# Weight sums two per projection step, and every on-chip pool at a multiple of 256 bytes

## The chip, the cores and the metric

The kernel runs on one core of one Trainium2 chip. The metric is the device time of one execution in microseconds; of several timed executions the median is given. The core has TensorE (PE, with its weight loads as PEld), VectorE (DVE), ScalarE (ACT) and GpSimd (POOL). SyncE (SP) issues nearly all loads from DRAM to the on-chip memory SBUF; POOL issues the DRAM-to-DRAM transfers of this kernel and a few small loads. All transfers run on the same 16 DMA engines, those of SP as queue q1 and those of POOL as queue q0.

## The reference, cut to what matters

One backbone layer on 512 latent tokens of width 1024, with 256 context tokens in front:

```
mod = silu(c) @ w_ada + b_ada            # six vectors: sh1, sc1, ga1, sh2, sc2, ga2
h   = modulate(rmsnorm(x), sh1, sc1)
x_a, b_a, c_a, q, k, v, r, lr_f, lr_b, gate_a, gate_b = split(h @ w_in + b_in)
y_a = (b_a * conv3(c_a * x_a)) @ w_conv_out
y_b = (rmsnorm(gla_bidir(q, k, v, ...)) * silu(r)) @ w_gla_out
y   = sigmoid(gate_a) * y_a + sigmoid(gate_b) * y_b
x   = x + ga1 * (y @ w_o)
x   = x + ga2 * (square(relu(modulate(rmsnorm(x), sh2, sc2) @ w_up)) @ w_down)
out = rmsnorm(x)
```

All data is float32. The MLP is 1024 to 4096 to 1024.

## The kernel before, in words

**Products.** Every operand of a large product is split into a high part (rounded to the fast float32 format, by ACT) and a low part (the rest, by DVE), and `mm3` makes three matmuls of it: high x high, high x low, low x high. A projection step is 8 blocks of the contraction, so 24 matmuls of 128 rows x 512 columns into one PSUM bank.

**Weights.** `weights(name, src)` takes a raw tile (`raw`, 4 of them, 4 KB per partition), lets SP load 512 KB into it (L125), and splits it into `h_<name>` (ACT) and `l_<name>` (DVE), of which there are 5 each. `Stream` asks for weights up to three steps ahead (`ahead` 3). Most weights are taken as columns, so each of their transfers is 1024 runs of 512 bytes.

**Order around the change.** `projections()` is a generator that yields after each of its 57 steps (i = 0 to 56): the 14 steps of the v and context keys, a query, 26 steps for the convolution branch (xa, c, b in turn, with two queries), 8 gates (`ga`), 8 of `co`. After each step the main loop (L923 to L928) advances the attention (`att`), then the weight sums (`sums`), and from step 44 on the second modulation (`mods`). The 16 steps of `gates()` (`r`, then `gb`) advance `mods` and `sums` too. A planner orders each engine's instructions by its own estimate of times; `pinned` ones keep the order of the program.

**Weight sums.** The down projection uses seven block products in place of eight, and so needs sums of quarters of `w_down`. `weight_sums()` makes them in DRAM, with 64 transfers of 512 KB that POOL issues: 16 copies from `w_down` (numbers 1 to 16), 16 accumulating transfers (17 to 32), then twice 8 copies of a sum into another (33 to 40 and 49 to 56) and 8 accumulating ones (41 to 48 and 57 to 64). Ahead of each stands a tiny copy (`tick`, L466) that reads the low part of the weights last asked for, so POOL waits at it, in order, until DVE has made that part:

```
for i, p, src, add in todo:
    pinned(nc.gpsimd.tensor_copy(out=tick, in_=latest[0][0:1, 0:1].bitcast(F32)))
    pinned(nc.gpsimd.dma_start(out=t_sum[i][p], in_=src, ...))       # accum_op add where add
    yield
```

`SUMS = (0, 1)` makes none at step 0 and one at each later step, 56 in `projections()`; the other 8 are made in `gates()`, one per step.

**Second modulation.** `ada_sum(i)` loads eight 512 KB blocks of `w_ada` (`wa`, L754) into the same four raw tiles as the weights, and DVE multiplies and adds them into two accumulators. `second_mods()` does so for shift 2, scale 2 and gate 1; a short product with a matrix of ones (`ps_ar`) then spreads the row over the partitions.

**Where the tiles lie.** The pools are laid one behind the other in each partition's memory: `const`, `wp` (raw, high and low weights), `kp` (the latent and MLP activations in split form, and 16 blocks of 2 KB), `sp` (columns of statistics, 1152 bytes), and `bp` (36 blocks of 2 KB), in whose place `mp` comes at the MLP. `const` begins 128 bytes past a multiple of 256 and takes 2976 bytes with each tile padded to 32. So `wp` and `kp`, whose sizes are multiples of 256, begin 32 bytes past a multiple of 256, and `bp` and `mp` 160 bytes past one. Every matrix operand of 512 columns starts at its pool's remainder.

Of the kernel before, what the change touches and what calls it, by code (L numbers as in the profile page):

```python
# [8 lines left out]
F32 = mybir.dt.float32  # L9
# [6 lines left out]
P = 128  # L16
# [23 lines left out]
NBLK = 36  # L40
NKEEP = 16
MODS_FROM = 44
SUMS = (0, 1)
UP_ORDER = [16 * j + 4 * g + i for g in range(4) for j in range(2) for i in range(4)]
TABLES = "natural_log_exp_and_others"

# [2 lines left out]
def hybrid_block_kernel(  # L49
# [9 lines left out]
    w_up, w_down, b_in, b_ada, out = w_up[0], w_down[0], b_in[0], b_ada[0], out[0]  # L59

    const = es.enter_context(tc.tile_pool(name="const", bufs=1))
    wp = es.enter_context(tc.tile_pool(name="wp", bufs=NW))
    kp = es.enter_context(tc.tile_pool(name="kp", bufs=NKEEP))
    sp = es.enter_context(tc.tile_pool(name="sp", bufs=4))
    pp = es.enter_context(tc.tile_pool(name="pp", bufs=8, space=bass.MemoryType.PSUM))
    dp = es.enter_context(tc.tile_pool(name="dp", bufs=1, space=bass.MemoryType.DRAM))

# [382 lines left out]

    t_sum = [[dp.tile([P, 2, 512], F32, tag=f"t{i}_{p}", name=f"t{i}_{p}") for p in range(NFF // 4)] for i in range(4)]
    tick = const.tile([1, 1], F32, name="tick")

    def quarter(j, hf, p):
        return rows(w_down, 16 * j + 2 * p, 512 * hf)

    def weight_sums():

        groups = range(NFF // 4)
        todo = [(i, p, quarter(0, i, p), False) for p in groups for i in range(2)]  # L460
        todo += [(i, p, quarter(i, 1, p), True) for p in groups for i in range(2)]
        for i, j, hf in ((2, 1, 1), (3, 1, 0)):
            todo += [(i, p, t_sum[(0, 2)[i - 2]][p], False) for p in groups]
            todo += [(i, p, quarter(j, hf, p), True) for p in groups]
        for i, p, src, add in todo:
            pinned(nc.gpsimd.tensor_copy(out=tick, in_=latest[0][0:1, 0:1].bitcast(F32)))  # L466
            pinned(nc.gpsimd.dma_start(out=t_sum[i][p], in_=src, **({"accum_op": ALU.add} if add else {})))  # L467
            yield
# [306 lines left out]
    def all_attention():  # L775
        for h in range(HEADS):
            yield from attention(h)
# [3 lines left out]
    def second_mods():  # L781
        yield from ada_sum(3)
        ps = psum("ps_ac")
        for k in range(KT):
            pe.matmul(ps[:, k:k + 1], ada[3][k // 4][:, (k % 4) * P:(k % 4 + 1) * P], ones[:, 0:1], start=True, stop=True)
        dve.tensor_copy(out=sh2, in_=ps[:, 0:KT])
        yield
        yield from ada_rows(4)
        for hf in range(2):
            g2 = blk("g2")  # L790
            nc.gpsimd.dma_start(out=g2, in_=g_norm2[0][hf * 512:(hf + 1) * 512].partition_broadcast(P))
            dve.scalar_tensor_tensor(out=ada[4][hf], in0=ada[4][hf], scalar=1.0, in1=g2, op0=ALU.add, op1=ALU.mult)
        yield from ada_rows(2)
# [110 lines left out]
    def gates():  # L904

        for j in range(KT):
            ps = project("r")
            rg = blk("rg")
            pinned(act.activation(out=rg, in_=ps, func=AF.Silu, bias=cb(40 + j)))
            pst = transposed("ps_ot", o_tok, j)  # L910
            dve.scalar_tensor_tensor(out=rg, in0=pst, scalar=ca(80 + j), in1=rg, op0=ALU.mult, op1=ALU.mult)
            og.append((blk(f"ogh_{j}", F32R), blk(f"ogl_{j}", F32R)))
            split(rg, *og[j])
            yield
        for j in range(KT):
            ps = project("gb")
            gb.append(kblk("gb"))
            pinned(act.activation(out=gb[j], in_=ps, func=AF.Sigmoid, bias=cb(56 + j)))
            yield
        pinned(nc.scalar.preload_act_table_set(TABLES))  # L920

    att, mods, sums = all_attention(), second_mods(), weight_sums()
    for i, _ in enumerate(projections()):  # L923
        next(att, None)
        for _ in range(SUMS[min(i, len(SUMS) - 1)]):
            next(sums, None)
# [3 lines left out]
        next(mods, None)  # L930
    for _ in gates():
        next(mods, None)
        next(sums, None)
    for _ in mods:
        pass
    for _ in sums:
# [291 lines left out]
```

## Time and profile before

| | us |
|---|---|
| median of 3 timed runs | 1000.24 (999.66 to 1001.4) |
| the profiled execution, whole | 1002.8 |
| its span, first to last instruction | 1001.0 |
| PE busy in it | 963.0 |
| DVE, ACT, POOL busy in it | 637.0, 487.8, 109.2 |
| mean granted PE clock | 0.989 of full speed |

Times of the trace count from the first instruction. A row of a timeline is start, duration, engine, line, operation, output <- inputs, count, and in brackets how long the engine sat idle before it and what ended that. Most rows name L81, the line of a helper through which all engines are called, so tiles tell more than lines. In the chain of waits a row is start, duration, engine and tile, and xN the number of instructions merged in it. PE instructions overlap, so the pace of a stream is the length of such a piece divided by its count.

### The profile page before, as it was taken

What the parts mean: (1) busy time and instruction counts of PE and PEld (TensorE: products, weight loads), DVE (VectorE), ACT (ScalarE), POOL (GpSimd) and SP (SyncE); (2) the same over time, 40 slices, a digit from 0 to 9 for tenths busy, and PEclk for the clock granted to TensorE, in tenths of its full rate; (3) what the DMA queues carried; (4) which work ended last, traced back from release to release, by engine and by line L of the source; (5) the groups of instructions that cost most, each with busy time, mean ns of one, the idle gap of its engine ahead of it and who ended that gap; (6) DMA issues with size and microseconds to landing.
All of it is one profiled execution on the core that took longest, in us unless ns stands there. A gap on an engine that the chain in (4) does not pass through costs nothing.

```text
span 1001.0 us, 13478 instructions
## 1 busy us (share of the span) xinstructions
PE 963.0 (96%) x4999; PEld 783.9 (78%) x4999; DVE 637.0 (64%) x1076; ACT 487.8 (49%) x862; POOL 109.2 (11%) x195
## 2 busy tenths in 40 slices
PE   3999999999999998799989999999999999999996
PEld 2678888778888887688878888898888888888875
DVE  5366676887688767666547354776332225699896
ACT  4465454645655474533334432374444344655662
POOL 7001021222211131002220000000000000000000
PEclk9999999999999999899989999999999999999998
DMA  9893154787664666855987425237533334555561
GB/s 264 231 289 127 33 190 138 164 169 164 144 167 146 172 129 154 244 169 175 251 205 235 129 98 171 61 89 234 162 85 105 95 116 142 192 179 191 179 211 42
DMA packets 160241, 161.22 MB, mean 161 GB/s; under 512 B 7268, under 2 KB 126160, under 8 KB 159920
## 3 DMA queue, kind: packets, MB, share of 16 engines
q1 hardware_dynamic: 146672, 123.89, 41.4%
q0 software_dynamic: 12928, 35.43, 15.1%
q10 hardware_dynamic: 576, 1.05, 0.3%
q8 instruction: 39, 0.64, 0.3%
q14 instruction: 26, 0.21, 0.1%
HBM read 158.25 MB, written 35.65 MB: 194 GB/s over the span
## 4 chain that ended last, share of the span: by engine, by line
PE 90%; DMA 4%; DVE 3%; SPq 1%; ACT 1%; issue 1%; DVEq 0%; ACTq 0%
PE ps_up L81 16%; PE ps_da L81 7%; PE ps_v L81 7%; PE ps_b L81 4%; PE ps_y L81 4%; PE ps_c L81 4%; PE ps_db L81 4%; PE ps_go L81 4%; PE ps_xa L81 4%; PE ps_gb L81 4%; PE ps_co L81 4%; PE ps_r L81 4%; PE ps_ga L81 2%; PE ps_dc L81 2%; DMA r_co<-in_w_conv_out_dram 2%; PE ps_k L81 2%
## 5 line engine op out<-in xcount | busy, mean ns | idle before, releaser
L81 DVE TENSOR_TENSOR l_up<-r_up,h_up 128x1024 fp32r<-128x1024 f32 x32 | 39.2, 1224 | 84.8 <-ACT h_up L81 84.7
L81 PE MATMUL ps_up<-h2h,l_up 128*128 128x512 f32 x232 | 90.3, 389 | 0.0
L81 PE MATMUL ps_up<-h2l,h_up 128*128 128x512 f32 x232 | 90.3, 389 | 0.0
L81 PE MATMUL ps_up<-h2h,h_up 128*128 128x512 f32 x232 | 90.3, 389 | 0.0
L81 DVE TENSOR_TENSOR l_dn<-r_dn,h_dn 128x1024 fp32r<-128x1024 f32 x56 | 68.4, 1222 | 27.1 <-ACT h_dn L81 26.9
L81 ACT CAST h_up<-r_up 128x1024 fp32r<-128x1024 f32 x32 | 33.6, 1053 | 78.8 <-PE ps_up L81 67.9
L81 ACT CAST h_dn<-r_dn 128x1024 fp32r<-128x1024 f32 x56 | 58.7, 1048 | 16.1 <-PE ps_up L81 16.1
L81 ACT CAST aph<-ug 128x512 fp32r<-128x512 f32 x56 | 34.8, 621 | 58.8 <-PE ps_da L81 25.6
L81 DVE SCALAR_TENSOR_TENSOR acc<-wa,silu_c,acc 128x512 f32<-128x512 f32 x64 | 45.4, 747 | 8.4 <-DMA wa<-in_w_ada_dram 8.2
L81 PEld LDWEIGHTS ps_up<-h2l,h_up 128*128 128x128 f32 x232 | 43.5, 188 | 9.1
L81 PEld LDWEIGHTS ps_up<-h2h,l_up 128*128 128x128 f32 x232 | 43.5, 188 | 9.0
L81 PEld LDWEIGHTS ps_up<-h2h,h_up 128*128 128x128 f32 x232 | 43.5, 188 | 9.0
L81 DVE TENSOR_TENSOR apl<-ug,aph 128x512 fp32r<-128x512 f32 x56 | 38.6, 689 | 13.5 <-ACT aph L81 13.2
L467 POOL DMA_DIRECT2D t<-in_w_down_dram x48 | 42.7, 905 | 3.8 <-issue 3.8
L81 PE MATMUL ps_da<-h_dn,aph 128*128 128x512 f32 x96 | 37.9, 395 | 0.0
L81 PE MATMUL ps_da<-h_dn,apl 128*128 128x512 f32 x96 | 37.9, 395 | 0.0
L81 PE MATMUL ps_da<-l_dn,aph 128*128 128x512 f32 x96 | 37.9, 394 | 0.0
L81 PE MATMUL ps_co<-yah,h_co 128*128 128x512 f32 x64 | 26.5, 413 | 0.0
L81 PE MATMUL ps_r<-hh,h_r 128*128 128x512 f32 x64 | 26.4, 412 | 0.0
L81 PE MATMUL ps_v<-h_v,hh 128*128 128x512 f32 x64 | 26.0, 406 | 0.0
L81 PE MATMUL ps_r<-hh,l_r 128*128 128x512 f32 x64 | 25.8, 402 | 0.0
L81 PE MATMUL ps_r<-hl,h_r 128*128 128x512 f32 x64 | 25.7, 401 | 0.0
(464 smaller groups left out, 2794.5 us busy)
## 6 DMA issues: line engine op xcount, KB each, us to landing
t<-in_w_down_dram POOLq DMA_DIRECT2D x48, 512.0 KB, 7.6
wa<-in_w_ada_dram SPq DMA_DIRECT2D x32, 512.0 KB, 4.8
r_up<-in_w_up_dram SPq DMA_DIRECT2D x32, 512.0 KB, 4.1
r_dn<-t SPq DMA_DIRECT2D x32, 512.0 KB, 3.5
r_dn<-in_w_down_dram SPq DMA_DIRECT2D x24, 512.0 KB, 3.6
wa<-in_w_ada_dram SPq DMA_DIRECT2D x32, 256.0 KB, 5.1
t<-t POOLq DMA_DIRECT2D x16, 512.0 KB, 5.3
r_v<-in_w_in_dram SPq DMA_DIRECT2D x8, 512.0 KB, 5.2
```

The costliest lines, as they stand in the source:

```text
L81: ins = op(*args, **kwargs)
L467: pinned(nc.gpsimd.dma_start(out=t_sum[i][p], in_=src, **({"accum_op": ALU.add} if add else {})))
```

## The change

After the change the main loop asks for no sum at step 0, for one at step 1 and for two at each later step. All 64 are then asked for by step 33, ahead of step 44 where the second modulation begins, and `gates()` asks for none. `sp` moves ahead of `wp`, and a pad of 96 bytes is added to `const`, which then takes 3072 bytes; `sp` with its 1152 bytes follows, so `wp`, `kp`, `bp` and `mp` all begin at multiples of 256 bytes.

```diff
-SUMS = (0, 1)
+PAD = 24
+SUMS = (0, 1, 2)
...
     const = es.enter_context(tc.tile_pool(name="const", bufs=1))
+    sp = es.enter_context(tc.tile_pool(name="sp", bufs=4))
     wp = es.enter_context(tc.tile_pool(name="wp", bufs=NW))
     kp = es.enter_context(tc.tile_pool(name="kp", bufs=NKEEP))
-    sp = es.enter_context(tc.tile_pool(name="sp", bufs=4))
...
     tick = const.tile([1, 1], F32, name="tick")
+    const.tile([P, PAD], F32, name="pad")
...
     for _ in gates():
         next(mods, None)
-        next(sums, None)
```

## Rows read from the trace of the kernel before

**Rows 1.** Page: mean busy share of the DMA engines, in tenths, 40 slices of 25 us

```profile
DMA  9893154787664666855987425237533334555561
```

**Rows 2.** PE timeline of the co and r stages, rows with idle time in brackets

```profile
386.44 0.69 PE L81 MATMUL ps_sl<-qt,kt 128*64 128x64 f32 x16 [1.76 <-DVE kt L81]
...
388.72 0.58 PE L81 MATMUL ps_s<-vcl,kwh 128*128 128x256 f32 x1 [1.28 <-DVE vcl L81]
...
414.67 1.12 PE L81 MATMUL ps_sl<-qt,kt 128*64 128x64 f32 x16 [5.01 <-DVE kt L81]
...
504.65 0.80 PE L81 MATMUL ps_ar<-ah,ones_r 128*128 128x512 f32 x1 [2.81 <-ACT ah L81]
```

**Rows 3.** ACT timeline of the same stages

```profile
382.81 1.05 ACT L81 CAST h_co<-r_co 128x1024 fp32r<-128x1024 f32 x1 [7.79 <-DMA r_co<-in_w_conv_out_dram]
...
410.70 1.04 ACT L81 CAST h_co<-r_co 128x1024 fp32r<-128x1024 f32 x1 [10.80 <-DMA r_co<-in_w_conv_out_dram]
...
489.83 1.05 ACT L81 CAST h_r<-r_r 128x1024 fp32r<-128x1024 f32 x1 [8.21 <-DMA r_r<-in_w_in_dram]
```

**Rows 4.** Windows: us, busy (x instructions) of PE, PEld, DVE, ACT, POOL, PEclk, DMA share, GB/s

```profile
398.60:402.00 3.40, 3.40 (x17) 2.81 (x16) 3.40 (x8) 1.30 (x3) 0.50 (x1) 1.00 0.86 186
...
422.50:429.30 6.80, 6.80 (x44) 5.26 (x43) 6.75 (x14) 4.22 (x9) 0.94 (x2) 1.00 0.34 96
...
514.70:521.40 6.70, 6.70 (x35) 5.53 (x32) 4.80 (x7) 3.72 (x6) 1.25 (x2) 1.00 0.75 159
```

**Rows 5.** DMA issues in 374:383, then in 395:411: count, size, median us to landing

```profile
r_co<-in_w_conv_out_dram SPq DMA_DIRECT2D x1, 512.0 KB, 8.6
...
r_co<-in_w_conv_out_dram SPq DMA_DIRECT2D x3, 512.0 KB, 10.9
```

**Rows 6.** DMA issues of the page, one weight of the convolution branch

```profile
r_c<-in_w_in_dram SPq DMA_DIRECT2D x8, 512.0 KB, 4.4
```

**Rows 7.** DMA queues: packets, MB, share; stretches 376:377, 490.5:492.5, 486:489 in turn

```profile
q0 software_dynamic: 96, 0.20, 109.8%
...
q1 hardware_dynamic: 1229, 0.62, 110.5%
...
q0 software_dynamic: 253, 0.49, 87.5%
q1 hardware_dynamic: 255, 0.17, 24.2%
```

**Rows 8.** POOL timeline, first and last tick of steps 13 to 17

```profile
164.43 1.04 POOL L466 COPY tick<-l_c 1x1 f32<-1x1 f32 x1 [30.32 <-DVE l_c L81]
...
181.53 0.24 POOL L466 COPY tick<-l_b 1x1 f32<-1x1 f32 x1 [6.12 <-DVE l_b L81]
```

**Rows 9.** SP timeline, the load of the query weights that comes next

```profile
165.46 0.37 SPq L125 DMA_DIRECT2D r_q<-in_w_in_dram  x1
```

**Rows 10.** ACT timeline, the casts of this load and of the xa behind it

```profile
185.33 1.03 ACT L81 CAST h_q<-r_q 128x1024 fp32r<-128x1024 f32 x1
...
191.37 1.05 ACT L81 CAST h_xa<-r_xa 128x1024 fp32r<-128x1024 f32 x1 [2.78 <-PE ps_b L81]
```

**Rows 11.** DVE, then PE timeline: a head's scores behind that cast

```profile
195.76 0.69 DVE L81 TENSOR_TENSOR kt<-kt,k 128x512 f32<-128x512 f32 x1
...
198.17 0.69 PE L81 MATMUL ps_sl<-qt,kt 128*64 128x64 f32 x16
```

**Rows 12.** Chain that ended last, long PE pieces: start, us, tile, matmuls

```profile
520.86 43.55 PE ps_gb L81 x192
565.34 44.62 PE ps_go L81 x192
609.95 33.60 PE ps_y L81 x144
...
730.19 0.93 PE ps_ar L81 x4
...
834.48 22.31 PE ps_db L81 x96
```

## The prediction

> **What bounds the kernel now.** I read the page first: of a span of 1001.0 us PE is busy for 963.0, and the DMA engines are busiest, at 0.9 or more, at the start and near 475 us [rows 1]. As a busy PE may be a waiting one, I next read the chain of waits. Nearly all of it is PE, in long pieces of matmuls at a fixed pace [rows 12]; only in the co stage (372 to 416 us) does it leave PE for a load, ACT and DVE. Third came the PE timeline for idle time inside that stage and in r, which the chain leaves at 495 us: 1.76, 1.28, 5.01 and 2.81 us [rows 2], 10.9 us in sum. Fourth came ACT, to see why: it takes its work in order, and a cast of weights that have not landed holds the attention's exponentials behind it. It stood 7.79 and 10.80 us before casts of co weights and 8.21 us before one of r [rows 3]. Those loads took 8.6 us and (median of three) 10.9 us [rows 5], against 4.4 us for the same shape elsewhere [rows 6]. [...] So the two stages hold 10.9 + 8.45 = 19.3 us that is not work. The rest is the pace of matmuls.
>
> **Part 1, the sums leave co and r.** At the old pace only 40 of the 64 sums have been issued when the first `wa` load goes out, near 340 us; the other 24 run among these loads, up to 516 us. After the change that stretch holds loads of weights and `wa` only. What a sum costs a load is in the queue rows: while both queues have work the engines serve them packet by packet, 253 of q0 against 255 of q1 in 3 us [rows 7], 84 per us each. Alone, q1 moves 1229 packets in 2 us, 614 per us, and q0 96 per us. A weight load of 1024 runs needs 1.7 us alone and 12.2 us beside accumulating transfers; with about 2.5 us of latency (4.4 less the 1.7) that is the 8.6 to 10.9 us seen. Without sums I take 4.5 to 6 us, as `wa` loads still share q1. ACT then stands some 3.5 to 4.5 us in co and 1 to 2 us in r, about half as long as now or less. How much wait PE forgives shows in the same rows: 7.79 us cost 1.76 + 1.28 and 10.80 cost 5.01, so 4.8 to 5.8 us is free. All three waits fall below that, so I count all idle time of rows 2 and the half clock as gone: 19.3 us, with 9 us as the low end should ACT be late from another cause. Next late is DVE in co, whose attention products come behind ACT's and then start 4 us sooner. POOL loses 8 ticks and 8 issues in `gates()`; its accumulator clears and bias loads for `mods` stood between them and can only come sooner.
>
> **Part 2, the sums enter steps 2 to 33.** Each added step pays one tick and one issue more on POOL. Its sequence of tick (0.24 to 1.04 us, [rows 8]) and an issue of about 1 us for an accumulating sum takes under 4 us for two in a 6.2 us step, so POOL keeps up. Behind POOL wait the clears of a head's two decay buffers, 2 or 3 us later once per head: nothing. The low tiles that a tick reads are free long before PE has used them, about 25 us on.
>
> The DMA engines are another matter. Up to step 12 (before 165 us) they take it: 23 sums in place of 12, where the engines were busy for 0.1 to 0.5 of the slices from 75 to 175 us [rows 1]. Steps 13 to 17, at 164.43 to 181.53 us [rows 8], then ask for ten sums, 24 to 33, nine of them accumulating where before five were asked for, four of them plain copies. Nine times 256 packets are 2304, or 27 us at 84 per us, from about 168.4 to 196 us. In these 27 us the loads get the same number of packets. The b load under way has some 700 packets left by then (an estimate: it is the next ahead of q in the queue), so q, issued at 165.46 [rows 9], is through after 1724 packets, at 189 us, and lands near 190; its cast is due at 185.33 [rows 10], 4.6 us before. xa, next in the queue, has 580 of its 1024 served by 196 and lands at about 198, due at 191.37. Here the cover is thin: the scores that follow the xa cast have their input at 195.76 + 0.69 and start at 198.17 [rows 11], 1.7 us later; behind q I take 1 us likewise. So PE stops 4.6 - 1 = 3.6 us, then about 1 us for what is left of xa, and with a low clock of 1.7 to 3.4 us behind it the burst costs 4.6 + 2.4 = 7 us. The bounds are 0 (the sums start later or spread, and the loads slip through) and 14 us (xa alone 12 us late, less 1.7, and 3.4 for the clock). The accumulating bursts of steps 21 to 25 and 29 to 33 have eight each, and loads there are issued some 24 us ahead of their cast, so 12.2 + 2.5 us fits: I take 0, at most 9 + 3.4 us for the first of them.
>
> **Part 3, the pools.** In rows 12 gb takes 43.55/192 = 226.8 ns a matmul and go 44.62/192 = 232.4. They have the same shape, format and clock. In gb both operands lie 32 bytes past a multiple of 256 (`wp`, `kp`); in go one lies at 32 and the other at 160 (`bp`). The slow pace, 232 to 233, is in db (22.31/96 = 232.4, `mp` with `wp`) and y (33.60/144 = 233.3) too. The alternative, that the far end of the memory is slower, is weakened by `ps_ar`: there `kp` meets a tile of `const` 128 past, both at the near end, at 0.93/4 = 232.5. So I take differing remainders as the cause, and afterwards there are none among these pools. Counting 512-column matmuls of differing remainders where PE is the limit: 660 in the down products x 5.6 = 3.7 us, go 192 x 5.6 = 1.1, y 192 x 6.5 = 1.25, co 144 (two of eight blocks lie in `kp`) x 5.6 = 0.8; together 6.8 us. The 96 of the keys wait for loads: 0. The bounds are 0 and 6.8; a loss has no row, since equal remainders never go above 226.8 in these.
>
> [...]
>
> **Sum.** 19.3 + 6.8 - 7 = 19.1 us, and 1 us for smaller waits on the same loads in the r and gb stages: 20 us. The trace comes from an execution of 1002.8 us, 1.8 more than its span, so that one would be 983. The median of the timed runs is 2.6 lower, 1000.24: I predict 980.
>
> **Rivals.**
> - The early bursts cost nothing. For it: until step 12 the engines have room, and the loads of later steps have 24 us. Against it: rows 9 and 10 give q 19.9 us, and the alternation of rows 7 needs more. 980 - 7 = 973 us.
> - The pace stays at 232 because nearness, not remainder, sets it. For it: every slow large product uses `bp` or `mp`. Against it: `ps_ar`, though only four matmuls. 980 + 7 = 987 us.
> - The co and r waits stay in half because raw tiles, not queues, make loads late: `wa` and weights share four, so a load goes out only when DVE has freed one. 980 + 10 = 990 us.
> - Slower: the accumulating bursts starve the convolution branch. One mechanism, the alternation; its place is 165 to 300 us; it decides from the point where a load takes over 24 us from issue to landing, when two loads wait in q1 as a burst begins. Three bursts of 12, 9 and 5 us with 3 us of low clock each are 35 us, against 26.1 gained: 1009 us. For it: the nine sums of steps 13 to 17. Against it: between the bursts come eight plain copies of few, large packets, in which q1 catches up, and late casts delay the ticks too.
>
> **How the numbers follow.** Forecast (975 to 986) 0.45, no early cost 0.17, pace unchanged 0.13, half the waits 0.14, starved 0.08, and 0.03 for a planner's new order that eats the gain. The rivals on the faster side and the first two on the slower lie within 968 to 996, which leaves out the starved case and the tails. About 0.2% (2 us) is what a measurement here can tell from no change: faster 0.89, same 0.03, slower 0.08.
>
> **What would show it.** Part 1: no PE idle of over 1 us in the co and r stages, casts of co waiting under 5 us, PEclk 1.00 throughout both. Part 2: q0 and q1 at equal counts near 170 to 195 us, an ACT wait before h_q or h_xa there, and a PE pause with low clock behind it. Part 3: go, y and db at 226 to 228 ns a matmul, a number that needs no other part. A PE pause in 200 to 300 us, or co casts still waiting 8 us with q0 empty, would make the prediction wrong.

## Result, and the profile after

The changed kernel takes 984.12 us (median of 4 runs, 983.62 to 984.98) against 1000.76 us of the kernel before beside it (999.66 to 1001.4): ratio 0.982, 95% interval 0.980 to 0.985. The profiled execution took 983.95 us, its span is 982.1. Forecast were 980 us, range 968 to 996. So the sign and the size came out, with errors inside that partly cancel.

The PE timeline (first v matmul) and the chain of waits (second ga product, gb) of both kernels give landmarks that split the 18.9 us of the span:

| stretch | before | after | difference |
|---|---|---|---|
| start to the first v matmul | 69.33 | 66.67 | -2.66 |
| to the second ga product | 284.22 | 292.36 | +8.14 |
| to gb (rest of ga, co, r) | 167.31 | 148.94 | -18.37 |
| gb to the end | 480.14 | 474.13 | -6.01 |

**The co and r stages.** First the page's clock and DMA lines (40 slices of 24.6 us), which answer to [rows 1]:

```profile
PEclk9999999989999999999999999999999999999999
DMA  9787196999697323733838225137433334656561
```

Then windows of the two stages, with the columns of [rows 4]:

```profile
375.00:425.00 50.00, 50.00 (x319) 40.19 (x318) 47.24 (x90) 32.79 (x65) 1.55 (x3) 1.00 0.54 159
500.00:525.00 25.00, 25.00 (x116) 20.66 (x115) 16.66 (x22) 9.67 (x12) 0.00 (x0) 1.00 0.57 170
```

PE is busy throughout both, and between them (125.00 of the 125 us from 375 to 500), at PEclk 1.00; none of the four pauses of [rows 2] is left. The loads of co weights and ACT's longest waits for a load before casts, which answer to [rows 5] and [rows 3] (DMA issues of 390 to 460 us, then ACT timeline):

```profile
r_co<-in_w_conv_out_dram SPq DMA_DIRECT2D x6, 512.0 KB, 4.3
```

```profile
393.78 1.05 ACT L82 CAST h_co<-r_co 128x1024 fp32r<-128x1024 f32 x1 [0.75 <-DMA r_co<-in_w_conv_out_dram]
...
462.96 1.05 ACT L82 CAST h_r<-r_r 128x1024 fp32r<-128x1024 f32 x1 [6.41 <-DMA r_r<-in_w_in_dram]
```

**The early stop.** The one slice with a lower clock, 196 to 221 us, holds a pause of PE. ACT, then PE, then the window around it (PEclk 0.77 is a mean: 1.00 up to 207.5 us, 0.50 from there to 214.3, of which 1.6 us are idle, then 1.00 again):

```profile
183.84 1.03 ACT L82 CAST h_q<-r_q 128x1024 fp32r<-128x1024 f32 x1
...
190.35 1.05 ACT L82 CAST h_xa<-r_xa 128x1024 fp32r<-128x1024 f32 x1 [3.24 <-DMA r_xa<-in_w_in_dram]
...
205.35 1.04 ACT L82 CAST h_c<-r_c 128x1024 fp32r<-128x1024 f32 x1 [11.03 <-DMA r_c<-in_w_in_dram]
```

```profile
209.08 1.12 PE L82 MATMUL ps_sl<-qt,kt 128*64 128x64 f32 x16 [4.65 <-DVE kt L82]
```

```profile
204.00:219.00 15.00, 10.35 (x61) 7.96 (x60) 10.93 (x21) 7.61 (x15) 5.86 (x8) 0.77 0.94 280
```

Neither the q nor the xa load stopped PE, but the c load behind them. The chain has it as one piece of 32.51 us, from its issue:

```profile
172.77 32.51 DMA r_c<-in_w_in_dram
```

The queues of 170 to 197 us, then of 197 to 203 us (packets, MB, share of 16 engines), show why:

```profile
q0 software_dynamic: 2295, 4.78, 91.2%
q1 hardware_dynamic: 2293, 1.16, 21.4%
...
q0 software_dynamic: 137, 2.17, 97.7%
q1 hardware_dynamic: 148, 0.07, 4.9%
```

For 27 us each queue gets the same number of packets, 85 per us, as in [rows 7]. In the next 6 us the plain copies of one sum into another begin, whose packets have 32 KB (66 packets of over 8 KB hold nearly all of q0's 2.17 MB), and the loads get 25 packets per us: still one for one, but each turn of q0 lasts longer (by the shares shown, a packet of q0 holds an engine for 0.68 us in the mean, against 0.17 in the 27 us before).

**The pace.** The chain's long pieces, which answer to [rows 12]:

```profile
507.97 43.59 PE ps_gb L82 x192
...
552.49 43.52 PE ps_go L82 x192
596.02 32.64 PE ps_y L82 x144
...
715.07 0.94 PE ps_ar L82 x4
...
819.37 21.76 PE ps_db L82 x96
```

go, y and db all take 226.7 ns a matmul now; `ps_ar`, whose two operands now lie 128 bytes apart in their remainder, stays at 0.94/4 = 235, though over four matmuls only.

### The profile page after: what moved, and what is told of

Its sections match the earlier page's. It is cut to its first block, busy times and chain, and to the rows that moved or that the text cites. A ratio compares the mean times of both kernels' runs of the same rounds, so it can differ in the third digit from the quotient of the medians.

```text
span 982.1 us, 13441 instructions
## 1 busy us (share of the span) xinstructions
PE 951.9 (97%) x4999; PEld 779.9 (79%) x4999; DVE 636.7 (65%) x1076; ACT 487.9 (50%) x862; POOL 109.6 (11%) x195
## 4 chain that ended last, share of the span: by engine, by line
PE 88%; DMA 6%; DVE 3%; SPq 1%; ACT 1%; issue 1%; POOL 0%; DVEq 0%; ACTq 0%; POOLq 0%
PE ps_up L82 16%; PE ps_da L82 7%; PE ps_v L82 5%; PE ps_co L82 5%; PE ps_ga L82 5%; PE ps_r L82 4%; PE ps_gb L82 4%; PE ps_y L82 4%; PE ps_go L82 4%; PE ps_db L82 4%; PE ps_b L82 4%; PE ps_c L82 3%; PE ps_xa L82 3%; DMA r_c<-in_w_in_dram 3%; PE ps_dc L82 2%; PE ps_k L82 2%
## 5 line engine op out<-in xcount | busy, mean ns | idle before, releaser
L82 DVE TENSOR_TENSOR apl<-ug,aph 128x512 fp32r<-128x512 f32 x56 | 38.5, 688 | 11.5 <-ACT aph L82 11.5
L752 POOL MEMSET acc<- 128x512 f32 x8 | 4.2, 527 | 202.8 <-DVE yl L82 100.3
L82 PE MATMUL ps_b<-hh,h_b 128*128 128x512 f32 x64 | 26.5, 414 | 0.0
L82 PE MATMUL ps_b<-hl,h_b 128*128 128x512 f32 x64 | 25.7, 401 | 0.0
L82 PE MATMUL ps_b<-hh,l_b 128*128 128x512 f32 x64 | 25.7, 401 | 0.0
```

Of the source, the lines that this page charges most:

```text
L82: ins = op(*args, **kwargs)
L752: nc.gpsimd.memset(acc[hf], 0.0)
```

## Experiments

Ratios are to the kernel before on the same chip; where it was slower than above (1002.6 to 1002.9), compare ratios and not times.

**e1: the pools alone.**

```diff
-SUMS = (0, 1, 2)
+SUMS = (0, 1)
...
         next(mods, None)
+        next(sums, None)
```

> The pools alone: sums as before, all large pools at multiples of 256 bytes. Theory (the starting remainders of the two operands set the matmul pace): go, y and db run at 226.7 ns a matmul, ps_ar stays near 233, and the time falls by the 6.4 us that the pieces of go, y, co and the down products lost in the changed kernel; co and r keep their pauses (about 10.9 us idle) and their low clock. If the 2.65 us by which the changed kernel started its first v products earlier also come from where the tiles lie, the fall is 9 us, to 991 to 992; if that was chance or came from the sums, it is 6.4, to 994. Rival (the pace changed because the order of instructions did): go and db stay at 232.4 ns and the time is 1000.

Measured: 994.91 us, ratio 0.993 (0.990 to 0.995), some 7 us. The chain's pieces, then PE in co:

```profile
561.31 43.52 PE ps_go L82 x192
...
828.18 21.76 PE ps_db L82 x96
```

```profile
410.34 1.12 PE L82 MATMUL ps_sl<-qt,kt 128*64 128x64 f32 x16 [6.01 <-DVE kt L82]
```

The pace follows the pools and the pause of co stays with the sums, so neither needs the other. The first v matmul starts at 66.80 us, as after the change, but the 7 us are little more than the 6.4 forecast for the pace alone. What the start-up owes to the pools is taken up at the end.

**e2: the sums alone** (the kernel before with the new `SUMS` and without the sums in `gates()`).

```diff
-SUMS = (0, 1)
+SUMS = (0, 1, 2)
...
         next(mods, None)
-        next(sums, None)
```

> The sums alone: two per step, pools where they were. Theory: the pauses of co and r go (17.5 us in the changed kernel), a stall near 204 us with low clock behind it comes (8.1 us up to ga), so the time falls by 9.4 us to 991; go, y and db stay at 232.4 ns a matmul. With the pools' 9 us this adds up to the 18.9 us of both. First v products at 69.9 us after the start if the start-up gain belongs to the pools, at 67.2 if it belongs to the sums. Rival (the two parts depend on each other): less than 6 or more than 13 us here.

Measured: 991.94 us, ratio 0.990 (0.988 to 0.992), some 10 us; with e1's 7 that is the whole change. The chain's pieces keep the old pace:

```profile
554.60 44.62 PE ps_go L81 x192
...
823.74 22.31 PE ps_db L81 x96
```

The c load takes 32.62 us again. The first v matmul starts at 68.38 us, between the 66.67 of the change and the 69.33 before it.

**e3: equal remainders that are not zero.**

```diff
-PAD = 24
+PAD = 32
```

> The changed kernel with the pad 32 bytes longer: wp, kp, bp and mp all begin 32 bytes past a multiple of 256, equal among themselves and at no multiple. Theory (only the difference of the two remainders counts for the matmul pace): go, y, db at 226.7 ns as in the changed kernel. Rival (an operand must lie at a multiple of 256): they rise to 232 or more and the time by 6 us or more, gb too. For the start-up: if loads gain from destinations at multiples of 256, the first v products come at 69.9 us and the time is 984 + 2.7 = 986.8; if not, at 67.2 and the time is 984.

Measured: 985.97 us, ratio 0.984 (0.981 to 0.986), not to be told from the changed kernel's.

```profile
554.69 43.52 PE ps_go L82 x192
...
821.54 21.76 PE ps_db L82 x96
```

The pace needs equal remainders, not zero ones: the rival falls. The first v matmul comes at 68.84 us, most of the way back to 69.33.

**e4: differences of 64 and 32 bytes.**

```diff
+    es.enter_context(tc.tile_pool(name="pd", bufs=1)).tile([P, 16], F32, name="pad1")
     bp = tc.alloc_tile_pool(name="bp", bufs=NBLK)
...
     mp = es.enter_context(tc.tile_pool(name="mp", bufs=1, reuse_waits="tile"))
+    mp.tile([P, 56], F32, tag="pad2", name="pad2")
```

> The changed kernel with bp 64 bytes past a multiple of 256 and mp 32 past one, wp and kp at 0. go and y then have operands that differ by 64, da, db, dc and dd by 32; before, both differed by 128. Theory A (any difference of remainders mod 256 costs): go, y and db at 232.4 ns. Theory B (only the bit of 128 counts): both at 226.7. Theory C (the cost grows with the difference): db between, nearer to 226.7, go behind it.

Measured: 990.43 us in a single execution.

```profile
553.00 43.96 PE ps_go L83 x192
596.96 33.60 PE ps_y L83 x144
...
821.56 22.39 PE ps_db L83 x96
```

That is 229.0 ns for go (64 bytes apart), 233.3 for y (64) and 233.2 for db (32). Every difference tried costs, which is theory A but for go; theories B and C fall, since 32 bytes cost as much as 128. Why go pays less than y at the same 64 bytes is open. They differ in their roles: in go the operand of 512 columns is the tile at 64 and the held one the weights at 0, in y and db it is the other way round.

These runs don't tell what the remainder is to be taken of: `wp` and `kp` are multiples of 2 KB long, so pools that agree modulo 256 bytes here agree modulo 512 too.

**e5: copies between sums in smaller packets.**

```diff
-    t_sum = [[dp.tile([P, 2, 512], F32, tag=f"t{i}_{p}", name=f"t{i}_{p}") for p in range(NFF // 4)] for i in range(4)]
+    t_sum = [[dp.tile([P, 2, 516], F32, tag=f"t{i}_{p}", name=f"t{i}_{p}")[:, :, 0:512] for p in range(NFF // 4)] for i in range(4)]
```

> The changed kernel with the DRAM sums in rows of 516 numbers, of which 512 are used: a copy of one sum into another then moves in 2-KB packets in place of 32-KB ones; nothing else is moved in time. Theory (packet by packet, so what sits beside a load is counted in packets, and each lasts as long as it is big): the c load that landed at 205.3 us got only 143 packets from 197 to 203 us because 32-KB packets alternated with its 512-byte ones; beside 2-KB packets it gets some 85 per us and lands 3 to 4 us sooner, at 201 to 202; the stop of PE at 204 falls from 5.04 us to 1 or 2, the low clock behind it shrinks or goes, and the time falls by 3 to 6 us against the changed kernel, to 978 to 981. Rival (the nine accumulating transfers alone make it late): landing at 204 to 206, stop of 4 us or more, 984.

Measured: 981.48 us, ratio 0.980 (0.977 to 0.982), whose interval meets the changed kernel's. The queues of 197 to 203 us, then PE:

```profile
q0 software_dynamic: 493, 1.67, 87.2%
q1 hardware_dynamic: 493, 0.24, 18.5%
```

```profile
207.68 0.69 PE L82 MATMUL ps_sl<-qt,kt 128*64 128x64 f32 x16 [1.96 <-DVE kt L82]
...
215.22 0.69 PE L82 MATMUL ps_sl<-qt,kt 128*64 128x64 f32 x16 [1.19 <-DVE kt L82]
```

The copies move in packets of 4 KB (375 of q0's 493), not in the 2 KB of the forecast. The loads get 493 packets where they got 148, the c cast comes 29.9 us after the load's issue (203.95 less 174.06) in place of 32.6, and one pause of 4.65 us becomes two of 1.96 and 1.19. So the wide packets add some 2.7 us to the load; the rest of the delay is the accumulating transfers'. The landing lies between the two forecasts, the shorter stop is the theory's. The low clock goes with the longer pause (granted in 200 to 225 us: 0.86 after the change, 1.00 in e5).

The edit does something else as well: it moves the rows of the first 16 copies, which slows them (see e9), and a stop at 134 us comes with it:

```profile
133.85 0.93 PE L82 MATMUL ps_kwt<-ident,cw 128*128 128x128 f32 x4 [1.93 <-DVE cw L82]
```

Behind this one the clock did fall (0.93 granted in 125 to 150 us, 1.00 after the change), though 1.96 us at 207 left it alone: the length of a pause doesn't tell by itself. In idle time and low clock the stop takes back some 3 us of the 4 that the shorter one at 204 gives, so the time of e5 doesn't price the wide packets.

**e6: sums 17 to 32 as plain copies.**

```diff
-    todo += [(i, p, quarter(i, 1, p), True) for p in groups for i in range(2)]
+    todo += [(i, p, quarter(i, 1, p), False) for p in groups for i in range(2)]
```

> The changed kernel with sums 17 to 32 as plain copies: it leaves out these additions. Theory (packets of the accumulating transfers, 2 KB where plain copies have 4 KB, so 256 in place of 128 per sum): the burst from 170 to 197 us halves, the c load lands by 195 us and PE has no stop of over 1 us at 204; its slice of 25 us loses 6.7 us, so 977. Rival (raw tiles or POOL make the load late, not packets in the queue): the stop stays.

Measured: 975.02 us in a single execution. The queues of 170 to 197 us:

```profile
q0 software_dynamic: 1083, 5.70, 59.6%
q1 hardware_dynamic: 5331, 2.68, 35.8%
```

With more bytes in q0 but half the packets, the loads get 5331 packets where they got 2293, the c cast waits for no load, and PE has no stop there. Raw tiles and POOL are as they were, so the rival falls.

**e7: the sums where the queues are empty.**

```diff
-SUMS = (0, 1, 2)
+SUMS = (0,) + (4,) * 6 + (2,) * 7 + (1,)
```

> The changed kernel with the sums put where the queues are empty: four at each of steps 1 to 6, two at each of 7 to 13, then one per step, all issued by step 39, ahead of step 44. Theory: 24 sums run from 72 us to some 118 us, when the loads of weights want nothing; 14 more from 120 to 160; from 165 us on one accumulating transfer per 6.2 us costs 2.7 us of the queue, as in the kernel before, whose PE had no stop there. The stop at 204 goes (6.7 us): 977 to 978. Rival (the burst goes before the v weights and their bias, so PE stops in the v stage near 120 to 140 instead): a stop of 2 us or more there, 980 to 986.

Measured: 983.38 us, ratio 0.980 (0.978 to 0.982): the rival's time. The stop at 204 us has gone, and another has come (DVE, then PE):

```profile
137.01 0.69 DVE L82 TENSOR_TENSOR v<-ps_v,vb 128x512 f32<-128x512 f32 x1 [4.67 <-DMA vb<-in_b_in_dram]
```

```profile
139.96 1.18 PE L82 MATMUL ps_kwt<-ident,cw 128*128 128x128 f32 x4 [3.86 <-DVE cw L82]
```

`vb`, the second half of the v bias, is loaded by POOL. It was issued at 124.73 us, behind two ticks that waited until 122.3 for a v weight, and landed 12.2 us later, behind two sums of its own queue.

**e8: no sums at step 7.**

```diff
-SUMS = (0, 1, 2)
+SUMS = (0,) + (4,) * 6 + (0,) + (2,) * 6 + (1,)
```

> The schedule of e7 without sums at step 7, so that no tick stands ahead of the second load of the v bias on POOL: four sums at steps 1 to 6, none at 7, two at 8 to 13, then one per step, all by step 41. Theory (that load stood behind ticks that wait for the low part of a v weight, and behind two sums in its own queue): it is issued before 122 us, lands by 128, PE's stop of 4.1 us at 136 and the low clock behind it go, and e7's slice from 125 to 150 us loses some 5 to 6 us: 977 to 978. Rival (the other sums beside it make it late, wherever it is issued): it lands after 132 us, the stop stays at 3 us or more, 982 to 983.

Measured: 976.26 us, ratio 0.975 (0.972 to 0.977). The issue of `vb` (median us to landing), then windows of the two places:

```profile
vb<-in_b_in_dram POOLq DMA_DIRECT2D x1, 256.0 KB, 19.2
```

```profile
125.00:150.00 25.00, 25.00 (x143) 20.96 (x142) 18.26 (x42) 10.00 (x24) 10.24 (x20) 1.00 1.06 204
200.00:225.00 25.00, 25.00 (x162) 19.78 (x161) 20.62 (x39) 12.62 (x25) 4.78 (x7) 1.00 0.78 156
```

`vb` takes 19.2 us, yet it was issued at 107.33, lands at 126.5 and is wanted at 129. Neither stop is left.

**e9: e8 with e5's rows of 516 numbers.**

> The kernel of e8 with the DRAM sums in rows of 516 numbers, so that no copy moves 32-KB packets. Theory: with one sum per step from 165 us on, a 32-KB copy holds a load back by some 3 us at most, which the loads can take; so within 1 us of e8. Rival (wide packets still cost in the convolution branch): 2 us or more below e8.

Measured: 982.44 us, ratio 0.981 (0.978 to 0.983): outside both forecasts.

```profile
vb<-in_b_in_dram POOLq DMA_DIRECT2D x1, 256.0 KB, 21.8
```

```profile
139.40 1.18 PE L82 MATMUL ps_kwt<-ident,cw 128*128 128x128 f32 x4 [5.96 <-DVE cw L82]
```

The edit also moves the rows of the first 16 copies, now 2064 bytes apart in place of 2048, which I had overlooked. Queue q0 in 78 to 92 us, when it has such copies alone, of e8 and of e9:

```profile
q0 software_dynamic: 1252, 4.56, 101.8%
```

```profile
q0 software_dynamic: 970, 3.51, 102.7%
```

The packets keep their size (3.6 KB in the mean), but 69 come per us in place of 89; why is not shown. The 24 early sums then take longer: POOL issues the last at 111.92 us in place of 104.45 and `vb` behind it at 114.61 in place of 107.33. `vb` lands at 136.4, and PE stops for 6 us. What the wide copies cost in e8 is not told by it.

**e10: the changed kernel beside e8.**

> The changed kernel itself, unaltered, beside e8 and e9 on one chip, so that these can be compared with it: 984 us again, ratio 0.982 to before, with the stop of 5 us at 204. By the theory e8 lies 6 us below it, by the rival 1 to 2.

Measured: 985.55 us, ratio 0.982 (0.980 to 0.985), the c load 32.62 us again. e8 lies 9.3 us below it on the same chip, where the theory had 6 and the rival 1 to 2; 1.3 of it comes by an earlier first v matmul (66.01 against 67.33), and most of the rest is the stop near 205 us (4.74 us idle) with its low clock (512-column matmuls 427 ns apart behind it, 211.78 to 215.62 us), which e8 doesn't have (PEclk 1.00 above). The ratio's interval of e8 is clear of this one.

## Why the prediction was right, point by point

- **What bounds the kernel.** Right: the pauses of co and r were waits on loads beside sums, e1 keeps them and e2 has none.
- **Part 1.** Forecast 19.3 us and 1 for smaller waits. Measured from the second ga product to gb: 18.37, of which about 0.7 is the pace in co; so 17.7, the mechanism right and the size 2.6 too large. The mis-sized term is the clock. No run shows the 8.45 us of low clock in the forecast: the three stretches of [rows 4] ran at PEclk 1.00, and the 0.50 in the first is POOL's busy time. What the trace shows are three stretches of about the same lengths at PEclk 0.50 that lie some 10 us earlier, partly in the idle time itself (columns of [rows 4]):

```profile
388.20:391.50 3.30, 2.78 (x12) 2.78 (x13) 3.30 (x8) 1.04 (x4) 0.00 (x0) 0.50 0.23 63
412.10:418.80 6.70, 4.13 (x23) 3.42 (x24) 6.61 (x13) 6.67 (x14) 0.97 (x2) 0.50 0.72 239
504.30:511.00 6.70, 6.34 (x14) 4.67 (x15) 1.71 (x3) 0.82 (x2) 0.79 (x1) 0.50 1.09 276
```

PE is busy for 13.25 us of these, and about half of that is lost: 6.6 us by the PEclk, 6.2 by the pace in the third, where 512-column matmuls start 427 ns apart (506.90 to 510.74 us, nine intervals) against 227 at PEclk 1.00. That is less than 8.45: the rest was counted as idle time already. With 10.86 of idle time the 6.6 make 17.5, which is what was measured (co 11.5 counted so and 11.4 measured; r, from its first product to gb, 6.0 and 6.2). The extra 1 us for smaller waits did not show. Casts of co wait for a load 0.75 us at most, where 3.5 to 4.5 were forecast, but one of r still waited 6.41 where 1 to 2 were forecast. PE lost nothing there, so the cover at that place is more than the 4.8 to 5.8 us taken over from co.

- **Part 2.** Forecast +7 us. Measured from the first v matmul to ga: +8.14. The alternation and its duration are as forecast (2295 packets of q0 in 27 us; counted were 2304). The step that failed is which load pays. q was to land at 190 and landed before its cast at 183.84; xa, due at 191.37, was 3.24 us awaited and did no harm; the c load behind them, which the prediction did not follow, paid. The term behind this is the estimate of 700 packets of the b load still ahead of q. The b load was through at 169 us, as the burst began, and q, next in the queue, landed at 178 (DMA issues, b at 162.82, q at 163.96):

```profile
r_b<-in_w_in_dram SPq DMA_DIRECT2D x1, 512.0 KB, 6.2
```

```profile
r_q<-in_w_in_dram SPq DMA_DIRECT2D x1, 512.0 KB, 14.2
```

By its own sign ("a PE pause in 200 to 300 us") the prediction was wrong here: the pause ended at 209.08. It is the burst of steps 13 to 17, one load later than forecast, and not a new one. Its worth (4.65 us idle, and 2.6 us, half of the 5.2 us of work at PEclk 0.50) came near 7 by luck. No run shows as such the 1.7 to 3.4 us of low clock in this sum, in its bounds and in the slower rival; measured were the 2.6 us. The rival's counter-argument, that q1 catches up beside "eight plain copies of few, large packets", was wrong for 197 to 203 us: beside these it is slowest, 25 packets per us. Some 0.6 us more is idle time of PE near 133 us behind the v bias. "Raw tiles, not queues" fell in the co stage and in e6; the starvation from 165 to 300 us was one stop, not three.

- **Part 3.** Forecast 6.8 us. Measured: go 1.10, y with its two late pieces 1.19, the down products 3.7, co about 0.7: 6.7 us. e1, e3 and e4 show differing remainders as the cause and rule out nearness; the modulus is open (e4).
- **Not forecast.** The start-up, 2.66 us faster (see below). It made up for most of what part 1 fell short and part 2 overran: without it the span would have gained 16.2 us in place of the 20 summed up.
- **From the profile to the median.** I took 2.6 us off, since before's profiled execution lay that far above its median. After's did not (983.95 against 984.12). The forecast for the profiled execution, 983, was 1 us off; most of the 4 us between 980 and 984 is this step.

## What to carry to other kernels

Count transfers that share the DMA engines in packets, and in how long each lasts, rather than in bytes, and follow every load in the queue until it has drained: here the last one behind the burst paid (32.51 us from issue to landing), and loads in runs of 512 bytes got fewest packets beside very large ones (25 per us beside 32 KB, 85 beside 2 KB). When a profile shows how long a slow clock lasted, check the stretch's own PEclk, and count only the work in it: its idle part is in the idle time already (of 6.70 us at PEclk 0.50 in the co stage PE was busy for 4.13). When two operands feed PE at its limit, lay their pools at equal remainders modulo 256 bytes (in these runs modulo 512 as well; 226.7 to 227.0 ns a matmul in place of 229.0 to 233.3) and read the pace per matmul in the chain to see whether it worked. A queue that is moved to where the engines are idle also moves past whatever else is issued behind it; e8 gained 6 us over e7, by their ratios, by leaving one step free for one small load.

## What the runs showed of the hardware that was not expected

**Loads into pools at multiples of 256 bytes cost the DMA engines less.** Queue q1 in the first 70 us (packets, MB, share of 16 engines), of the kernel before, the changed kernel and e3:

```profile
q1 hardware_dynamic: 23761, 17.92, 86.9%
```

```profile
q1 hardware_dynamic: 24050, 18.48, 83.9%
```

```profile
q1 hardware_dynamic: 23840, 18.07, 88.0%
```

Divided: 4.85% per MB before, 4.54 after, 4.87 in e3, which differs from the changed kernel by 32 bytes of pad alone. With `wp` and `kp` at 32 bytes past a multiple (before, e2, e3) it is 4.85 to 4.89; at a multiple (the changed kernel, e1, e4 to e10) 4.52 to 4.63. That is 6 to 7% of these engines' time for each byte, from one trace of each kernel. What it is worth is less sure: the first v matmul starts at 68.38 to 69.33 us in the three, at 64.97 to 69.15 in the nine, 2 us earlier in the mean, and in one of them (e7) no earlier.

**The pace of a matmul depends on where its two operands lie to each other**: 226.7 to 227.0 ns at equal remainders, 0 or 32; 233.2 at 32 apart, 229.0 and 233.3 at 64, 232.4 and 233.3 at 128. What causes this is not shown.
